# One decode step in full precision: memory values formed by tokens, norm weights on ScalarE, selected value pages loaded by SyncE, and a shorter Newton step in the tail

## The chip, the cores and the metric

The kernel runs on 1 core of one Trainium2 chip. The metric is the device time of one execution in microseconds (us). The time before is the median of three runs.

## What is computed

One layer of a hybrid decoder is applied to 256 prompt tokens (one sequence) and to 32 new tokens (8 sequences of 4), all in float32, with D = 2048. The parts that matter here, cut from the reference:

```python
def rms_norm(x, g):
    y = xf * lax.rsqrt(jnp.mean(xf * xf, axis=-1, keepdims=True) + NORM_EPS)
    return y * g

mkv = (rms_norm(mem_prompt, mem_norm_g[l]) @ w_mem_kv[l]).reshape(1, 256, 2, 4, 128)   # memory keys, values: an output too
h = rms_norm(x, norm_g)
c_h, c_b, c_c, c_g, q, n_g, b_g, kv6, m_q, m_g = split_cols(h @ w_in)
o_cmp, o_sel = nsa_cmp_sel(q, q_rot, pos, k_cmp, v_cmp, k_sel, v_sel)   # v_sel: pages of the cache and new rows
o_m = gqa_attend(m_q, mem_kv[:, :, 0], mem_kv[:, :, 1], None)           # attention over 256 memory tokens
y_m = jax.nn.silu(m_g) * o_m
mixed = jnp.concatenate([y_a, y_b, y_m], axis=-1)
y = rms_norm(x + mixed @ w_out, final_g)
```

The cache of each of the 8 sequences holds 16 pages of 128 tokens, found through a page table.

## The kernel before

**Products.** Every large product is split for precision: a weight "half" (128 x 1024, 512 KB) is copied by ScalarE to a rounded high part (tile `wh`, `w_hi`, L228), VectorE subtracts to get the low part (`wl`, `w_lo`, L233), and TensorE runs 24 matmuls per half: 8 high times high, 8 high times low of the activation, 8 low times high (`product_half`, L250). Two halves make an output tile of 128 columns: weights are the stationary operand and the 256 memory tokens (or 288 tokens of x) stream past them, into a PSUM tile `z`. Raw halves are prefetched five deep (`w_load`, L221): the first 14 on SyncE's queue, all later ones on GpSimd's. All matmuls are recorded as L120, transposes as L125, all VectorE and ScalarE operations as L137, through helpers.

**The order of the work** is written by a Python planner. TensorE's stream is the main program; after every 12 matmuls it calls `chunk()`, which advances the other jobs (generators in `live`): normalization, rotary and softmax steps, and the stream of cache pages (`stage_stream`). A list `stages` gives each page use a due time, and `loading` with the costs in `ISSUE` estimates when a page is there. What comes out is a fixed order on each engine.

**Start.** The memory rows are squared and scaled by `mem_norm_g`, and w_mem's products run first: four tiles of memory keys, then four of memory values (tiles 4 to 7), each tile [128 channels x 256 tokens]. `mem_rstd` (L878) makes the reciprocal root mean square, spread over tokens in `Vc`. Key tiles go from PSUM to `mixed` by ScalarE and are scaled there by VectorE; value tiles are scaled by VectorE straight from PSUM into `mvt` (`mem_tile`, L1016), stored by a DMA (L898) and turned around by two TensorE transposes each (`mvtp`), since the attention needs tokens on partitions; ScalarE copies them to `mixed`.
Meanwhile `prep_x` (L930) makes the high and low parts of the normalized x: one VectorE SCALAR_TENSOR_TENSOR per 128 rows multiplies `rx` by `norm_g` and by the token's factor `rstd_x`, ScalarE writes the high part (`x<-rx`), VectorE subtracts. The first product of x (q, first head) comes right after the last value tile and the small product `bg`.

**The decode caches** pass through six 512 KB page buffers (`st`, and `qk` once the prompt's memory attention is over). SyncE loads compressed-branch pages (`ckc`, 256 KB each), selected keys (`ckk`, 128 KB each), window and memory rows; each page address is read from the page table into a register (`page_ids`, L333). The selected values are different: `selv_load` (L583, recorded as L584) is one GpSimd indirect DMA per 512 KB buffer, that is four pages, with row numbers in `rows_v`; there are 16 such loads for each half of the sequences. Four buffers make one group, used by 16 or more `od` matmuls. A SyncE DMA waits in its order for the one eight before it.

**End.** The first pass of the output projection (`y1`) runs as tiles and as row products `zr`; `split_y1` makes its operands, last the decode columns of the memory heads, and then the second pass. In the tail the last columns are formed by rows: z[0], z[1] for the prompt, and `zd` for the 32 decode tokens (`decode_rows`, L1544). For each of the three, the partial sum is added (`squares`, L1551), squared and summed by ScalarE, and `rsqrt` (L199) turns the sum into the factor r by a square root on ScalarE and a Newton step on VectorE; r is spread by a matmul (`rb`), and the output is scaled and stored (L1571, L1578).

Of the kernel before, what the change touches and what calls it, by code (L numbers as in the profile page):

```python
# [79 lines left out]
def decode_step(ctx, tc, xT, xN, xD, xL, fgl, memT, cst, w_in, w_mem, w_out, w_bg, pt, ptv, ckc, ckk, ckv, wk, wv, mk, mv,  # L80
                o_y, o_kv, o_mem, o_conv, o_wk, o_wv):
# [1680 lines left out]
```

## Time and profile before

| what | value |
|---|---|
| runs | 610.86, 612.21 and 616.13 us (median 612.21) |
| the profiled execution | 616.16 us |
| its span in the profile | 614.4 us |
| granted TensorE clock | 0.996 |
| HBM over the span | 184.74 MB read, 13.60 MB written |
| longest-busy engines after TensorE | VectorE 461.0 us, ScalarE 285.3 us, GpSimd 200.5 us |

In timeline rows the first number is the start in us from the span's start, the second the time up to the end of the row's last instruction, and "x16" counts instructions that the row joins. A bracket at the end gives idle time before the row and what ended it. Matmuls overlap, so their pace is read from start to start. In rows of groups, the numbers behind the bar are total busy us and mean ns of one, then the idle time before them. SPq and POOLq rows are DMA issues on SyncE and GpSimd.

### The profile page before, as it was taken

How to read it: one execution, taken by the hardware profiler on the slowest of the kernel's cores; microseconds unless marked ns; L12 is line 12 of the kernel's file. 1: busy time of each engine (PE TensorE's matmuls, PEld its weight loads, DVE VectorE, ACT ScalarE, POOL GpSimd, SP SyncE). 2: the span in 40 equal slices, each digit the busy share in tenths (PEclk: the TensorE clock that was granted, in tenths of full speed). 3: DMA queues.
4: the chain of work that ended last, by engine and by line, in shares of the span. 5: the costliest groups of instructions: out<-in, count | busy, mean ns of one | idle time of the engine just before them, and what ended most of it. 6: DMA issues, size and time to landing. Idle time of an engine off the chain costs nothing.

```text
span 614.4 us, 13419 instructions
## 1 busy us (share of the span) xinstructions
PE 603.0 (98%) x4919; PEld 554.0 (90%) x4919; DVE 461.0 (75%) x749; ACT 285.3 (46%) x499; POOL 200.5 (33%) x282
## 2 busy tenths in 40 slices
PE   8999999999999999999999999999999999999997
PEld 5999999989799999989889889899889989889995
DVE  4879899988485779989789888897668733357666
ACT  4755445543355444435334434543543544335552
POOL 2012544533124442433453552323111336222200
PEclk8999999999999999999999999999999999999999
DMA  8999798999968999798878898999899998859834
GB/s 285 394 403 404 258 320 300 345 310 337 365 203 280 370 407 375 250 387 298 310 232 313 284 386 273 309 318 311 289 334 332 336 353 291 288 195 411 281 130 155
DMA packets 76226, 190.85 MB, mean 311 GB/s; under 512 B 8896, under 2 KB 26464, under 8 KB 75904
## 3 DMA queue, kind: packets, MB, share of 16 engines
q0 software_dynamic: 26048, 100.48, 46.0%
q1 hardware_dynamic: 49104, 88.25, 40.4%
q10 hardware_dynamic: 1008, 1.25, 0.6%
q8 instruction: 39, 0.64, 0.4%
q14 instruction: 27, 0.22, 0.1%
HBM read 184.74 MB, written 13.60 MB: 323 GB/s over the span
## 4 chain that ended last, share of the span: by engine, by line
PE 78%; DMA 11%; DVE 8%; issue 2%; SPq 1%; ACT 0%; ACTq 0%; DVEq 0%
PE z L120 56%; DMA st<-ckc 5%; PE zr L120 4%; PE od L120 3%; DMA st<-ckk 3%; PE sk L120 3%; PE zf L120 2%; DVE wl L137 2%; DVE pooled L137 2%; PE acc L120 2%; PE s L120 2%; DMA rx<-xT 1%; DVE st L137 1%; PE pt L125 1%; DMA mraw<-memT 1%
## 5 line engine op out<-in xcount | busy, mean ns | idle before, releaser
L120 PE MATMUL z<-x,wh 128*128 128x288 f32 x1664 | 254.4, 302 | 0.0
L137 DVE TENSOR_TENSOR wl<-w,wh 128x1024 fp32r<-128x1024 f32 x147 | 185.7, 1265 | 84.6 <-PE z L120 34.9
L120 PEld LDWEIGHTS z<-x,wh 128*128 128x128 f32 x1664 | 229.7, 188 | 7.8 <-issue 6.1
L137 ACT ACTIVATE wh<-w 128x1024 fp32r<-128x1024 f32 x148 | 154.3, 1052 | 25.1 <-PE z L120 15.4
L120 PE MATMUL z<-x,wl 128*128 128x288 f32 x832 | 127.2, 295 | 0.3 <-DVE wl L137 0.3
L120 PEld LDWEIGHTS z<-x,wl 128*128 128x128 f32 x832 | 115.7, 188 | 0.8 <-DVE wl L137 0.7
L356 POOL TENSOR_TENSOR st<-st,cst 128x512 f32<-128x512 f32 x63 | 69.3, 1102 | 133.8 <-DVE st L137 49.3
L225 POOL DMA_DIRECT2D w<-w_in x104 | 58.2, 560 | 109.1 <-DVE wl L137 82.4
L137 DVE TENSOR_REDUCE pooled<-st 128x16 f32<-128x1024 f32 x63 | 76.2, 1210 | 5.8 <-POOL st L356 5.8
L137 DVE TENSOR_TENSOR st<-st,cst 128x512 f32<-128x512 f32 x63 | 43.3, 688 | 10.9 <-DMA st<-ckc 10.8
L225 POOL DMA_DIRECT2D w<-w_out x32 | 17.5, 550 | 63.0 <-DVE wl L137 43.1
L584 POOL DMA_INDIRECT st<-ckv,rows_v x26 | 27.1, 1042 | 31.9 <-PE od L120 17.4
L137 ACT ACTIVATE P<-P,nm 128x128 f32<-128x128 f32 (+1 forms) x32 | 14.2, 445 | 29.3 <-DVE nm L137 29.3
L120 PE MATMUL z<-m,wh 128*128 128x256 f32 x192 | 27.3, 287 | 0.5 <-DVE mvt L137 0.5
L120 PE MATMUL z<-y,wh 128*128 128x288 f32 x192 | 27.6, 297 | 0.0
L120 PE MATMUL z<-y1a,wh 128*128 128x288 f32 x168 | 26.7, 299 | 0.0
L120 PEld LDWEIGHTS z<-y,wh 128*128 128x128 f32 x192 | 26.3, 188 | 0.1
L120 PEld LDWEIGHTS z<-y1a,wh 128*128 128x128 f32 x168 | 23.6, 188 | 2.1 <-issue 1.2
L120 PEld LDWEIGHTS z<-m,wh 128*128 128x128 f32 x192 | 24.7, 191 | 0.8 <-issue 0.7
L120 PE MATMUL sk<-st,qz 128*32 128x256 f32 x272 | 20.4, 383 | 1.4 <-DMA st<-ckk 1.2
L120 PE MATMUL od<-st,S 128*32 128x256 f32 x256 | 18.7, 382 | 0.0
L120 PE MATMUL zf<-mixed,w 128*128 128x256 f32 x64 | 16.6, 421 | 1.9 <-DVE mixed L137 1.7
(318 smaller groups left out, 716.2 us busy)
## 6 DMA issues: line engine op xcount, KB each, us to landing
w<-w_in POOLq DMA_DIRECT2D x104, 512.0 KB
st<-ckc SPq DMA_DIRECT2D x126, 256.0 KB, 5.8
w<-w_out POOLq DMA_DIRECT2D x32, 512.0 KB
st<-ckk SPq DMA_DIRECT2D x112, 128.0 KB, 5.1
w<-w_mem SPq DMA_DIRECT2D x12, 512.0 KB, 7.1
o_wk<-wk POOLq DMA_DIRECT2D x8, 512.0 KB
o_wv<-wv POOLq DMA_DIRECT2D x8, 512.0 KB
st<-mv SPq DMA_DIRECT2D x7, 512.0 KB, 7.9
```

What stands on the lines that cost most here:

```text
L120: nc.tensor.matmul(out, a, b, **kw)
L125: nc.tensor.transpose(out, a, b)
L137: return getattr(self.engine, name)(*args, **kw)
L225: (nc.gpsimd if s >= ON_SYNC else nc.sync).dma_start(raws[s], wsrc[s])
L356: done.append(eng.tensor_tensor(tm[:, :, kv], tm[:, :, kv], acmp[:, kv].unsqueeze(1).unsqueeze(1).to_broadcast([128, 2, 4, 64]), op=ALU.mu ...
L584: nc.gpsimd.indirect_dma_start(t, None, ckv, bass.IndirectOffsetOnAxis(ap=rows_v[:, j * 4 + b:j * 4 + b + 1], axis=0))
```

## The change

It has six parts.

1. **Memory values by tokens** (`mem_values`). The four value products become one product in two PSUM tiles `zv` [128 tokens x 512 channels]: the memory block is stationary and 512 weight columns stream. A half is 12 matmuls of 128x512 in place of 24 of 128x256. The host lays out w_mem's second half accordingly. ScalarE writes both tiles to `mixed` with the token's factor `mr` as scale; two DMAs store them (`o_memv`, 256 KB each, on GpSimd's queue). The `mvt` multiplications, the eight transposes, their eight copies and four 128 KB stores are gone.
2. **Norm weights of x on ScalarE** (`x_scales`): 16 copies of 128x288 with `norm_g` as a per-partition scale, in place, in six groups, one group per half; VectorE then multiplies a whole group (128x864) by `rstd_x` at once.
3. **Selected values of the first half of the sequences** (`selp_load`): four SyncE DMAs per buffer, each a page's rows to 32 partitions with 4 KB each, in place of one indirect DMA. The second half keeps `selv_load`.
4. **`rsqrt` in the tail**: with constants scaled ahead (`rest` has six columns, one more VectorE operation), the step after the square root takes a reciprocal and two operations in place of a reciprocal and three.
5. **Decode rows**: the partial sum enters `zd` by a matmul with the identity, and ScalarE and VectorE read the PSUM tile; VectorE's addition for g = 2 is gone.
6. **Memory columns of `y1`**: `mem_out` calls the last step of `split_y1` itself, where `split_y1` polled for it before.

```diff
-ISSUE = {"cmp_load": 1.5, "selk_load": 3.75, "selv_load": 0.0}
+ISSUE = {"cmp_load": 1.5, "selk_load": 3.75, "selv_load": 0.0, "selp_load": 3.0}
...
     def rsqrt(r, ssq, rest=None):
 
         v, t = small(3, "yv", 1)[:, :r.shape[1]], small(3, "yt", 1)[:, :r.shape[1]]
-        act.activation(r, ssq, AF.Sqrt, scale=1.0 / D, bias=C("eps") if rest is None else rest)
-        if rest is None:
-            vec.tensor_scalar(v, ssq, 1.0 / D, EPS, op0=ALU.mult, op1=ALU.add)
-        else:
-            vec.scalar_tensor_tensor(v, ssq, 1.0 / D, rest, op0=ALU.mult, op1=ALU.add)
+        if rest is not None:
+            act.activation(r, ssq, AF.Sqrt, scale=1.0 / D, bias=rest[0])
+            vec.scalar_tensor_tensor(v, ssq, -0.5 / D, rest[1], op0=ALU.mult, op1=ALU.add)
+            vec.reciprocal(r, r)
+            vec.scalar_tensor_tensor(t, r, r, v, op0=ALU.mult, op1=ALU.mult)
+            vec.scalar_tensor_tensor(r, t, 1.5, r, op0=ALU.add, op1=ALU.mult)
+            return
+        act.activation(r, ssq, AF.Sqrt, scale=1.0 / D, bias=C("eps"))
+        vec.tensor_scalar(v, ssq, 1.0 / D, EPS, op0=ALU.mult, op1=ALU.add)
         vec.reciprocal(r, r)
         vec.tensor_tensor(t, r, r, op=ALU.mult)
         vec.scalar_tensor_tensor(t, t, -0.5, v, op0=ALU.mult, op1=ALU.mult)
...
         mm.sort(key=lambda x: x[0])
-        for n, (_, a, b) in enumerate(mm):
+        run_half(s, [(out, a, b, first and n == 0, last and n == 23) for n, (_, a, b) in enumerate(mm)], last)
+    def run_half(s, mm, last, between=None):
+        m = len(mm) // 2
+        for n, (out, a, b, start, stop) in enumerate(mm):
             if s == DIRECT and n == 0:
-            if n == LOAD_AT:
+            if n == LOAD_AT * m // 12:
                 w_load(s + WR + 1)
                 next(x_next, None)
-            matmul(out, a, b, start=(first and n == 0), stop=(last and n == 23))
-            if n == 23 and LOW_FIRST <= s < NH - 18:
+                if s > 5:
+                    next(x_scale, None)
+            matmul(out, a, b, start=start, stop=stop)
+            if n == 2 * m - 1 and LOW_FIRST <= s < NH - 18:
                 w_lo(s + 2)
-            if n % 12 == 11 and not (last and n == 23):
+            if n == 7 and between:
+                between()
+            if n == m - 1:
+                chunk()
+            if n == 2 * m - 1 and not last:
                 chunk()
...
+    def mem_values():
+        z = [pz.tile([128, 512], F32, name=f"zv{tt}", tag="z") for tt in range(2)]
+        def out(tt):
+            planes = mixed[:, 12 + 2 * tt:14 + 2 * tt, 0:256]
+            act.activation(planes, z[tt].rearrange("p (a n) -> p a n", a=2), AF.Copy, scale=mr[:, tt:tt + 1])
+            nc.gpsimd.dma_start(o_memv[tt].rearrange("p (a n) -> p a n", a=2), planes)
+
+        for h in range(8):
+            s = nhalf[0]
+            nhalf[0] += 1
+            w_hi(s + 2)
+            w_lo(s + 1)
+            wh, wl = his.pop(s), los.pop(s)
+            mm = []
+            for tt in range(2):
+                for k in range(2):
+                    hi, lo = (m_hl[n][:, 2 * h + k, tt * 128:(tt + 1) * 128] for n in range(2))
+                    w = slice(k * 512, (k + 1) * 512)
+                    early = 2 * tt + (k if h == 7 and tt else 0)
+                    mm += [(early, tt, hi, wh[:, w]), (early, tt, lo, wh[:, w]), (2.5 if h == 7 and not tt else 4, tt, hi, wl[:, w])]
+            mm.sort(key=lambda x: x[0])
+            i = [[n for n, x in enumerate(mm) if x[1] == tt] for tt in range(2)]
+            run_half(s, [(z[tt], a, b, h == 0 and n == i[tt][0], h == 7 and n == i[tt][-1]) for n, (_, tt, a, b) in enumerate(mm)],
+                     h == 7, (lambda: out(0)) if h == 7 else None)
+        assert "rstd_m" in env
+        out(1)
+        chunk()
...
+    def selp_load(j, b, t):
+        src = ckv.rearrange("(a p) c -> a p c", p=32)
+        for i, v in enumerate(page_ids(128 + j * 16 + b * 4, 4)):
+            nc.sync.dma_start(t[32 * i:32 * i + 32, :], src[ds(v, 1)].rearrange("a p c -> (a p) c"))
...
         env["mem_decoded"] = True
+        if "rest" in y1:
+            while env.get("gated", 0) < 4:
+                yield 1
+            y1["rest"]()
...
-    stages += spread(*T_V0, some(winv_load, winv_use, 0, 1) + some(selv_load, selv_use, 0, 4))
+    stages += spread(*T_V0, some(winv_load, winv_use, 0, 1) + some(selp_load, selv_use, 0, 4))
...
+    def x_scales():
+        for i in range(6):
+            yield
+            k, t = xg[i]
+            for j in range(t.shape[1] // NT):
+                act.activation(xr[k + j], xr[k + j], AF.Copy, scale=C("ng")[:, k + j:k + j + 1])
+
+    x_scale = x_scales()
...
+        for i in range(4):
             while i not in mem_raw:
                 yield 1
-            dst = mem_raw[i]
-            if i < 4:
-                vec.tensor_tensor(dst, dst, rstd_m, op=ALU.mult)
-            yield 1
-            if i == 3:
-                nc.gpsimd.dma_start(o_mem[0:4].rearrange("m p n -> p m n"), mkT)
-            if i >= 4:
-                nc.gpsimd.dma_start(o_mem[i], dst)
-                yield 2
-                t = ptr.tile([128, 512], F32, name=f"mvtp{i}", tag="t")
-                for s in range(2):
-                    transpose(t[:, s * 128:(s + 1) * 128], dst[:, s * 128:(s + 1) * 128], ident)
-                for s in range(2):
-                    act.activation(mvn(s, i - 4), t[:, s * 128:(s + 1) * 128], AF.Copy)
+            vec.tensor_tensor(mem_raw[i], mem_raw[i], rstd_m, op=ALU.mult)
+            yield 1
+        nc.gpsimd.dma_start(o_mem.rearrange("m p n -> p m n"), mkT)
...
-        g, r = C("ng"), rstd_x
+        r = rstd_x
         flat = lambda t, k, n: t[:, k:k + n, :].rearrange("p k n -> p (k n)")
         for i in range(len(xg) + 1):
             if i < len(xg):
                 k, x = xg[i]
                 n = x.shape[1] // NT
-                for j in range(k, k + n):
-                    vec.scalar_tensor_tensor(xr[j], xr[j], g[:, j:j + 1], r, op0=ALU.mult, op1=ALU.mult)
+                xv = x.rearrange("p (k n) -> p k n", n=NT)
+                vec.tensor_tensor(xv, xv, r.unsqueeze(1).to_broadcast([128, n, NT]), op=ALU.mult)
                 act.activation(flat(x_hl[0], k, n), x, AF.Copy)
...
     def mem_tile(i, z):
-        dst = mkT[:, i, :] if i < 4 else zt("A", "mvt")[:, :256]
-        if i < 4:
-            act.activation(dst, z, AF.Copy)
-        else:
-            yield 2
-            assert "rstd_m" in env
-            vec.tensor_tensor(dst, z, rstd_m, op=ALU.mult)
-        mem_raw[i] = dst
+        act.activation(mkT[:, i, :], z, AF.Copy)
+        mem_raw[i] = mkT[:, i, :]
+        return
+        yield
...
         then(mem_tile(i, z))
-    for i in range(2, 8):
+    for i in range(2, 4):
         then(mem_tile(i, proj(*m_hl, 256)))
+    mem_values()
...
-        while not env.get("mem_decoded"):
-            yield 1
...
+        def rest():
...
+            y1["done"] = True
+
+        y1["rest"] = rest
+        if env.get("mem_decoded"):
+            rest()
...
                 matmul(zd[32 * q:32 * q + 32, :128], mixed[:, k, 256:NT], wr[k // 2][:, o:o + 128],
-                       start=(k == 0), stop=(k == KT - 1), skip_group_check=True)
-
-    def squares(g, z):
-        vec.tensor_tensor(part[g], z, part[g], op=ALU.add)
-        act.activation(scratch[:, :part[g].shape[1]], part[g], AF.Square, accum_out=sums2[:, g:g + 1])
+                       start=False, stop=(k == KT - 1), skip_group_check=True)
+
+    y_of = [part[0], part[1], zd[:, :128]]
+
+    def squares(g):
+        if g < 2:
+            vec.tensor_tensor(part[g], z[g], part[g], op=ALU.add)
+        act.activation(scratch[:, :part[g].shape[1]], y_of[g], AF.Square, accum_out=sums2[:, g:g + 1])
     def gains(g):
-        vec.tensor_tensor(out[g][:, out[g].shape[1] - part[g].shape[1]:], part[g], fgr[g], op=ALU.mult)
+        vec.tensor_tensor(out[g][:, out[g].shape[1] - part[g].shape[1]:], y_of[g], fgr[g], op=ALU.mult)
         r = small(1, f"yr{g}", 1)
-        rsqrt(r, ssq, rest[:, g:g + 1])
+        rsqrt(r, ssq, (rest[:, g:g + 1], rest[:, 3 + g:4 + g]))
...
+    vec.tensor_scalar(rest[:, 0:3], ssq[:, 0:3], 1.0 / D, EPS, op0=ALU.mult, op1=ALU.add)
+    vec.tensor_scalar(rest[:, 3:6], ssq[:, 0:3], -0.5 / D, -0.5 * EPS, op0=ALU.mult, op1=ALU.add)
+    squares(0)
...
+    matmul(zd[:, :128], ident, part[2], start=True, stop=False, skip_group_check=True)
     decode_rows(0, SPREAD_AT)
...
-    squares(2, zd[:, :128])
```

The planner puts out a new order. The places below are those where it differs most beside the diff.

ScalarE, from the sixth value half on. `wh` is a high weight part, `x` a high part of x, `mixed<-mvtp` a transposed value tile. Before:

```order
L137 ACTIVATE wh_558<-w_411 128x1024
L137 ACTIVATE x_112<-rx 128x864
L137 ACTIVATE wh_603<-w_455 128x1024
L137 ACTIVATE mixed<-mvtp_619 128x128 x2
L137 ACTIVATE x_112<-rx_413 128x864
L137 ACTIVATE wh_651<-w_504 128x1024
L137 ACTIVATE x_112<-rx_457 128x288
L137 ACTIVATE wh_694<-w_552 128x1024
L137 ACTIVATE mixed<-mvtp_710 128x128 x2
L137 ACTIVATE wh_738<-w_595 128x1024
```

After; `rx<-rx,cst` are the copies with `norm_g`, `mixed<-zv` the two value tiles:

```order
L137 ACTIVATE rx_413<-rx_413,cst 128x288 x3
L137 ACTIVATE wh_557<-w_448 128x1024
L137 ACTIVATE x_112<-rx_413 128x864
L137 ACTIVATE rx_450<-rx_450,cst 128x288
L137 ACTIVATE wh_586<-w_484 128x1024
L137 ACTIVATE x_112<-rx_450 128x288
L137 ACTIVATE wh_614<-w_518 128x1024
L137 ACTIVATE wh_640<-w_549 128x1024
L137 ACTIVATE mixed<-zv_427,mr 128x2x256
L137 ACTIVATE mixed<-zv_428,mr 128x2x256
L137 ACTIVATE wh_667<-w_580 128x1024
L137 ACTIVATE bgT<-bg 128x288
```

The weight halves of the first product of x (`wh_614` and `wh_640`) now stand ahead of the two value evictions, and the norm-weight copies between the weight copies.

TensorE, the end of the value products and the first product of x (`z_794`). Before:

```order
L120 MATMUL z_693<-m_111,wh_651 128x256
L120 MATMUL z_693<-m_110,wl_696 128x256 x8
L120 MATMUL bg<-rx_249,qmz 32x288 x3
L120 MATMUL bg<-rx,qmz 32x288 x9
L120 MATMUL bg<-rx_413,qmz 32x288 x3
L120 MATMUL bg<-rx_457,qmz 32x288
L120 MATMUL z_794<-x_112,wh_694 128x288
L120 MATMUL z_794<-x_113,wh_694 128x288
```

After:

```order
L120 MATMUL zv_428<-wh_586,m_110 128x512
L120 MATMUL zv_428<-wh_586,m_111 128x512
L120 MATMUL zv_427<-wl_616,m_110 128x512 x2
L120 MATMUL zv_428<-wh_586,m_110 128x512
L120 MATMUL zv_428<-wh_586,m_111 128x512
L120 MATMUL zv_428<-wl_616,m_110 128x512 x2
L120 MATMUL z_666<-x_112,wh_614 128x288
L120 MATMUL z_666<-x_113,wh_614 128x288
```

The tile `zv_427` ends four matmuls before `zv_428`, and the first product of x (now `z_666`) follows at once; `bg` (16 matmuls) now comes after its first 12 matmuls, where it stood ahead of that product. The four pairs of transposes `mvtp` that stood inside the halves before this place and after it are gone.

The loads of selected values, one buffer group's start. Before, on GpSimd (`w` is a weight load, `st<-st,cst` a multiplication for a compressed page):

```order
L356 TENSOR_TENSOR st_107<-st_107,cst 128x2x256
L225 DMA w_3824<-w_in 128x1024
L584 DMA st_108<-ckv,rows_v 128x1024
L584 DMA st_104<-ckv,rows_v 128x1024
L584 DMA qk_793<-ckv,rows_v 128x1024
L584 DMA st_105<-ckv,rows_v 128x1024
L356 TENSOR_TENSOR st_106<-st_106,cst 128x2x256
L225 DMA w_3900<-w_in 128x1024
L225 DMA w_3965<-w_in 128x1024
```

After, on SyncE, the start of the first of the four buffers (ISA sets up a register):

```order
L387 ISA
L387 DMA st_105<-ckc 128x512
L387 ISA
L387 DMA st_105<-ckc 128x512
L379 TENSOR_LOAD ptt
L631 ISA
L631 DMA st_106<-ckv 32x1024
```

The pair of ISA and DMA comes four times for each buffer, behind one table read. So a group has 16 DMAs in SyncE's order, ahead of the `ckc` pages that follow; GpSimd's order has no `ckv` row until the second half of the sequences.

More of the change, by code (lines that the diff above doesn't have):

```diff
@@ L80, in decode_step @@
 def decode_step(ctx, tc, xT, xN, xD, xL, fgl, memT, cst, w_in, w_mem, w_out, w_bg, pt, ptv, ckc, ckk, ckv, wk, wv, mk, mv,
-                o_y, o_kv, o_mem, o_conv, o_wk, o_wv):
+                o_y, o_kv, o_mem, o_memv, o_conv, o_wk, o_wv):
     nc = tc.nc
@@ L680, in memv_use @@
         yield
+    y1 = {}
     def mem_out():
@@ L771, in decode_step @@
     rstd_m = Vc
+    mr = one.tile([128, 2], F32, name="mr")
     rstd_x = zt("C", "rstd_x")
@@ L917, in token_rstd @@
         yield lag
-        r = small(3, "yr")
         w = len(groups)
@@ L1131, in mem_gate @@
         vec.tensor_scalar(sg_m[:, h, :], sg[:, 256:NT], 0.5, None, op0=ALU.mult)
+        env["gated"] = h + 1
     def nsa_gate(h, z):
@@ L1401, in split_y1 @@
             vec.tensor_tensor(y1["lo"](j)[:, :n], mixed[:, j, :n], y1["hi"](j)[:, :n].bitcast(F32), op=ALU.subtract)
-        while not env.get("mem_decoded"):
-            yield 1
-        m = mixed[:, 4:8, 256:NT]
-        vec.tensor_tensor(m, m, sg_m, op=ALU.mult)
-        act.activation(a[:, 4:8, 256:NT], m, AF.Copy)
-        for lo, j in ((a[:, 12:14, 256:NT], 4), (b[:, :, 256:NT], 6)):
-            vec.tensor_tensor(lo, mixed[:, j:j + 2, 256:NT], a[:, j:j + 2, 256:NT].bitcast(F32), op=ALU.subtract)
-        y1["done"] = True
+        def rest():
+            m = mixed[:, 4:8, 256:NT]
+            vec.tensor_tensor(m, m, sg_m, op=ALU.mult)
+            act.activation(a[:, 4:8, 256:NT], m, AF.Copy)
+            for lo, j in ((a[:, 12:14, 256:NT], 4), (b[:, :, 256:NT], 6)):
+                vec.tensor_tensor(lo, mixed[:, j:j + 2, 256:NT], a[:, j:j + 2, 256:NT].bitcast(F32), op=ALU.subtract)
+            y1["done"] = True
+        y1["rest"] = rest
+        if env.get("mem_decoded"):
+            rest()
     spawn(split_y1(), 2)
@@ L1530, in decode_step @@
     out = (yo[:, 0:2048], yo[:, 2048:4096], yod)
-    rest, sums2 = small(3, "yrest", 1), small(3, "ysums", 1)
+    rest, sums2 = small(6, "yrest", 1), small(3, "ysums", 1)
     quarters = small(32, "imp", 1)
@@ L1600, in decode_step @@
     rows(z[0], ws[2], 6, y, 0, False, True)
-    vec.tensor_scalar(rest, ssq[:, 0:3], 1.0 / D, EPS, op0=ALU.mult, op1=ALU.add)
-    squares(0, z[0])
+    vec.tensor_scalar(rest[:, 0:3], ssq[:, 0:3], 1.0 / D, EPS, op0=ALU.mult, op1=ALU.add)
+    vec.tensor_scalar(rest[:, 3:6], ssq[:, 0:3], -0.5 / D, -0.5 * EPS, op0=ALU.mult, op1=ALU.add)
+    squares(0)
     gains(0)
@@ L1611, in decode_step @@
     scale_tiles(0, 4, 8, nc.sync)
-    squares(1, z[1])
+    squares(1)
     scale_tiles(0, 8, 12, nc.sync)
@@ L1620, in decode_step @@
     scale_tiles(1, 0, 4, nc.sync)
-    squares(2, zd[:, :128])
+    squares(2)
     busy(TAIL_BUSY[0])
@@ L1677, in _ktiles, with _kpairs @@
     return w.reshape(KT, 128, n, 128).transpose(2, 1, 0, 3).reshape(n, 128, KT * 128)
+def _kpairs(w):
+    return w.reshape(4, 4, 128, 512).transpose(0, 2, 1, 3).reshape(4, 128, 2048)
 def _inputs(x_prompt, x_sample, cache_kv, cache_win, state_conv, cache_mem, page_table, mem_prompt,
@@ L1716, in _inputs @@
     pt = np.concatenate([page_table.reshape(2, 4, 8, 2).transpose(0, 2, 1, 3).reshape(1, 128),
-                         page_table.reshape(2, 4, 16).transpose(0, 2, 1).reshape(1, 128)], 1)
+                         page_table.reshape(2, 4, 4, 4).transpose(0, 2, 1, 3).reshape(1, 128)], 1)
     ptv = page_table.reshape(2, 4, 4, 4).transpose(3, 0, 2, 1).reshape(4, 32).repeat(32, 0)
@@ L1720, in _inputs @@
                 memT=A(np.concatenate([vec(mem_norm_g), tr(mem_prompt.reshape(256, D)).reshape(128, KT * 256)], 1)), cst=A(cst), w_in=A(_ktiles(wcat)),
-                w_mem=A(_ktiles(w_mem_kv[0])), w_out=A(np.concatenate([_ktiles(wo[:, :128 * DT]), wl.transpose(0, 2, 1, 3).reshape(4, 128, 2048)], 0)), w_bg=A(wbg), pt=A(pt), ptv=A(ptv), ckc=A(ckc), ckk=A(ckk), ckv=A(ckv),
+                w_mem=A(np.concatenate([_ktiles(w_mem_kv[0][:, :512]), _kpairs(w_mem_kv[0][:, 512:])])), w_out=A(np.concatenate([_ktiles(wo[:, :128 * DT]), wl.transpose(0, 2, 1, 3).reshape(4, 128, 2048)], 0)), w_bg=A(wbg), pt=A(pt), ptv=A(ptv), ckc=A(ckc), ckk=A(ckk), ckv=A(ckv),
                 wk=A(wk), wv=A(wv), mk=A(mk), mv=A(mv))
-_OUTS = dict(o_y=(128, KT * NT), o_kv=(12, 128, NT), o_mem=(8, 128, 256), o_conv=(128, 72), o_wk=(4, 2, 128, 1024),
+_OUTS = dict(o_y=(128, KT * NT), o_kv=(12, 128, NT), o_mem=(4, 128, 256), o_memv=(2, 128, 512), o_conv=(128, 72), o_wk=(4, 2, 128, 1024),
              o_wv=(2, 4, 128, 1024))
@@ L1744, in _outputs @@
             A(kv[:NTP, 4:6])[None, None], A(conv[0:2])[None, None],
-            A(r["o_mem"].reshape(2, 4, 128, 256).transpose(3, 0, 1, 2))[None, None],
+            A(np.stack([r["o_mem"].transpose(2, 0, 1), r["o_memv"].reshape(256, 4, 128)], 1))[None, None],
             A(kv[NTP:, 0:4]).reshape(1, 8, 4, 4, 2, 128), A(win)[None], A(conv[2:18]).reshape(1, 8, 2, 512))
```

6 lines of the change are left out of this document (2 added, 4 removed).

## Prediction

> **What bounds the kernel now.** I read the page's busy table first, then the chain of waits that ended last, then TensorE's waits.
>
> ```profile
> PE 603.0 (98%) x4919; PEld 554.0 (90%) x4919; DVE 461.0 (75%) x749; ACT 285.3 (46%) x499; POOL 200.5 (33%) x282
> PE 78%; DMA 11%; DVE 8%; issue 2%; SPq 1%; ACT 0%; ACTq 0%; DVEq 0%
> ```
>
> ```profile
> PE zf L120 <- DVE mixed L137: 1.7, 2, 1.4
> PE sk L120 <- DMA st<-ckk: 1.2, 1, 1.2
> PE pt L125 <- DVE P L137: 1.2, 1, 1.2
> PE z L120 <- DVE mvt L137: 0.5, 1, 0.5
> ```
>
> TensorE is busy 603.0 of 614.4 us. The rows of its waits show total, count and longest: between the first products and the tail hardly 4 us are waits. So the bound is TensorE's own work, and an edit pays if it takes matmuls out, closes one of these few waits, or shortens the tail behind the last matmul. Work taken from VectorE (75% busy) or GpSimd (33%) pays nothing by itself, and every new wait of TensorE costs its full length.
>
> **Memory values by tokens.** TensorE's timeline over the eight halves of the value products:
>
> ```profile
> 35.87 1.69 PE L120 MATMUL z<-m,wh 128*128 128x256 f32 x12
> 45.03 2.08 PE L120 MATMUL z<-m,wh 128*128 128x256 f32 x16
> 47.91 1.60 PE L120 MATMUL z<-m,wh 128*128 128x256 f32 x12
> 49.35 0.38 PE L125 MATMUL mvtp<-cst,mvt 128*128 128x128 f32 x2
> 51.00 2.08 PE L120 MATMUL z<-m,wh 128*128 128x256 f32 x16
> 52.92 1.18 PE L120 MATMUL z<-m,wl 128*128 128x256 f32 x8
> 54.59 1.66 PE L120 MATMUL z<-m,wh 128*128 128x256 f32 x12 [0.50 <-DVE mvt L137]
> 60.70 2.15 PE L120 MATMUL bg<-rx,qmz 128*32 128x288 f32 x32
> ```
>
> An undisturbed half of 24 matmuls takes 47.91 - 45.03 = 2.88 us, so 0.120 us for each 256-wide matmul. For the 512-wide form the row products near the end give the pace:
>
> ```profile
> 592.62 1.09 PE L120 MATMUL zr<-wh,y 128*128 128x512 f32 x4
> 594.01 1.09 PE L120 MATMUL zr<-wh,y 128*128 128x512 f32 x4
> ```
>
> Six lie between these starts (four of this row and two low ones), so 1.39 / 6 = 0.232 us each. Twelve make 2.78 us: 0.10 less per half, 8 x 0.10 = **0.8 us** in all. Halving the count saves little because the columns streamed stay the same. [...]
>
> The half that starts at 47.91 with a pair of transposes lasts to 51.00, 3.09 us or 0.21 more than one without. Four pairs go: **0.85 us**. The wait before 54.59 goes too: eight matmuls from 52.92 end at 52.92 + 8 x 0.12 = 53.88, so TensorE lost **0.7 us** until VectorE had read a PSUM tile; the new tiles are held through all eight halves and are not read in between. Together 2.35 us off a stretch that now lasts 60.70 - 35.87 = 24.8 us (0.4 of it is transposes that fall after 60.70).
>
> **What stands against it there.** First, the new order on ScalarE: the eviction of `zv_427` stands behind the weight copies for halves 16 and 17, and the first product of x needs that tile's buffer. ScalarE, VectorE and the pace of preparation before:
>
> ```profile
> 44.48 1.22 DVE L137 TENSOR_TENSOR wl<-w,wh 128x1024 fp32r<-128x1024 f32 x1
> 45.62 1.37 DVE L137 SCALAR_TENSOR_TENSOR rx<-rx,cst,rstd_x 128x288 f32<-128x288 f32 x3
> 47.24 1.05 DVE L137 TENSOR_TENSOR x<-rx,x 128x864 fp32r<-128x864 f32 x1
> 58.62 1.06 ACT L137 ACTIVATE wh<-w 128x1024 fp32r<-128x1024 f32 x1
> L137 ACT ACTIVATE ysum<-ysum,cst 128x288 f32<-128x288 f32 x12 | 6.4, 537 | 0.4
> L137 ACT ACTIVATE x<-rx 128x864 fp32r<-128x864 f32 x5 | 4.6, 928 | 7.9 <-DVE rx L137 7.9
> 49.72 0.53 POOL L225 DMA_DIRECT2D w<-w_in  x1 [1.55 <-DVE wl L137]
> ```
>
> The copy at 58.62 is that of half 17; its load was issued at 49.72, so it takes at most 8.9 us to land. With the halves 0.1 to 0.3 us shorter the load goes out near 48.6 and is there by 57.5 at the latest; the copy (1.06) ends by 58.6 and the eviction, 0.63 us for 512 columns like the ScalarE row of 128x512 quoted for the tail, by 59.2. Without a wait the first product of x would start at 60.70 - 0.8 - 0.42 - 0.7 = 58.8 (0.42 for the two transpose pairs before that point). That is a wait of 0 to 0.4 us, more if the load lands later than now; I take **0.3**, bounds 0 and 2.4 (2 us later).
>
> Second, the norm weights. The operation moved is not in the trace of before, but a ScalarE copy of the same shape with a per-partition scale is: 537 ns. Three cost at most 1.6 us, at least 3 x (928 / 864 x 288 = 309 ns) = 0.9. ScalarE then does per half about 1.06 + 0.93 + 1.3 = 3.3 us, and VectorE 1.22 + 1.05 + 1.05 = 3.3 (a 128x864 multiplication taken like the subtraction) where it had 1.22 + 1.37 + 1.05 = 3.6 and in every second half an `mvt`. TensorE needs 2.78 per half. So preparation is quicker than before and still slower than TensorE over the five halves in which it runs, 5 x 0.5 = 2.5 us of drift, against a lead of about two halves (low parts are made one half ahead and weights two). I take **0.2 us** of wait from this, with bounds 0 and 2.
>
> **Selected value pages.** GpSimd loses 16 operations on which TensorE does not wait; no gain. SyncE gets 64 page loads, and the `od` groups are read every 15 to 20 us. These rows show how fast SyncE brings pages now, how long they take to land, and how close the groups stand:
>
> ```profile
> 390.60 7.32 SPq L342 DMA_DIRECT2D st<-ckk  x12
> 425.21 13.73 SPq L342 DMA_DIRECT2D st<-ckk  x16
> 149.82 1.81 SPq L342 DMA_DIRECT2D st<-ckk  x3
> 160.20 1.02 PE L120 MATMUL sk<-st,qz 128*32 128x256 f32 x10 [1.24 <-DMA st<-ckk]
> st<-ckk SPq DMA_DIRECT2D x112, 128.0 KB, 5.1
> 293.48 0.66 PE L125 MATMUL pt<-cst,P 128*128 128x128 f32 x4
> 313.51 0.41 PE L120 MATMUL od<-st,S 128*32 128x256 f32 x2
> 352.30 1.87 PE L120 MATMUL z<-x,wh 128*128 128x288 f32 x12
> 367.55 0.42 PE L120 MATMUL od<-st,S 128*32 128x256 f32 x3
> ```
>
> Twelve key pages went out in 7.32 us (0.61 each), sixteen in 13.73 (0.86), and half of them land within 5.1 us. The first group has from 293.48 to 313.51, 20.0 us, for 16 x 0.61 to 0.86 + 5.1 = 14.9 to 18.9. The last has 367.55 - 352.30 = 15.25 us now; the new order puts 12 fewer 288-wide matmuls there (1.6 us), so 13.65, for 12 pages: 7.3 to 10.3 + 5.1 = 12.4 to 15.4. So the first three groups should be in time and the last is on the edge: I take **0.6 us** of wait, with bounds 0 and the rival below. A value page is 4 KB to each of 32 partitions, which no row shows; by bytes it is one of the key pages.
>
> [...]
>
> **The tail.** Rows from the last matmul to the last store:
>
> ```profile
> 601.72 0.49 PE L120 MATMUL rb<-cst,yr 128*128 128x128 f32 x2
> 599.84 0.63 ACT L137 ACTIVATE st<-ysum 128x512 f32<-128x512 f32 x1 [5.01 <-DVE ysum L137]
> 607.86 0.29 DVE L137 TENSOR_TENSOR ysum<-zd,ysum 128x128 f32<-128x128 f32 x1
> 608.19 0.31 ACT L137 ACTIVATE st<-ysum 128x128 f32<-128x128 f32 x1 [1.18 <-DVE ysum L137]
> 609.91 0.16 DVE L137 SCALAR_TENSOR_TENSOR yt<-yt,yv 128x1 f32<-128x1 f32 x1
> 610.11 0.16 DVE L137 SCALAR_TENSOR_TENSOR yr<-yt,yr 128x1 f32<-128x1 f32 x1
> ```
>
> The addition at 607.86 holds ScalarE's squares until 608.19; without it they start about 0.33 earlier. One Newton operation of the chain goes, 610.11 - 609.91 = 0.20. Against these stands the identity matmul, at most the 0.49 of the two 128x128 `rb` records at 601.72, at least 0.12 by the 256-wide pace; I take 0.2. Sum: 0.33 + 0.20 - 0.2 and about 0.2 from shorter waits of `rb` for the earlier factors: **0.5 us** gained, bounds 0 and 0.8. The last part (memory columns of `y1`) I cost at nothing: TensorE waits there for nothing now, and the row products it still has before those columns cover the chain; without that cover it is four operations of about 0.3 us (rows 607.86 and 608.19 have its size), 1.2 us.
>
> **Sum.** -0.8 - 0.85 - 0.7 + 0.3 + 0.2 + 0.6 - 0.5 = -1.75 us. The profiled 616.16 (span 614.4 and 1.76 around it) becomes 614.4; it ran 3.95 us above the median, so I carry the difference over to the median: 612.21 - 1.75, **610.5 us**.
>
> **Rivals.** (a) *Preparation becomes the bound in the value stretch*: the load of half 17 lands 2 us later than now, or the drift reaches TensorE by as much, so 2.4 in all. For it: this stretch, where VectorE is busy all the time and the DMA engines are full (columns PE, PEld, DVE, ACT, POOL, granted clock, DMA share, GB/s):
>
> ```profile
> 40.00:50.00 10.00, 10.00 (x86) 10.00 (x85) 10.00 (x18) 5.63 (x6) 3.20 (x6) 1.00 1.03 398
> ```
>
> Against it: VectorE's work per half falls. Then -2.35 + 2.4 + 0.6 - 0.5 = +0.15: 612.4.
>
> (b) *Slower: the value pages come late.* The place is `od`; the point is SyncE's pace: above (13.65 - 5.1) / 12 = 0.71 us per page the last group waits, above (20.0 - 5.1) / 16 = 0.93 the first too. The price: the third page row above ended at 151.63 and its user started at 160.20, so a page may need 8.6 us. With that and 0.86, a group of 16 needs 22.4 and one of 12 needs 18.9: late by 2.4 for the first, taken alike for the next two, and by 5.2 for the last, 12.4 us. With the rest (-2.35): 622.3. Against it: 5.1 is the median, and only one key group of the whole run waited, 1.24 us.
>
> (c) *More gain*: the new order also closes the waits of 1.2 and 1.2 for P and for key pages in the list above (GpSimd and VectorE have less ahead of them), and the pages cost nothing: -1.75 - 0.6 - 2.4 = -4.75: 607.5.
>
> (d) *It does not do what it says*: the 512-wide matmuls run no faster per column and the waits stay; only the transposes and the tail are won, -0.85 - 0.5 + 1.1: 612.0.
>
> **Chances.** Forecast 0.48, (a) 0.2, (b) 0.12, (c) 0.12, (d) 0.08. The likeliest case alone spans 609 to 612; 8 in 10 needs (c), (a) and (d), and the near part of (b): **606.3 to 615.5**. A measurement here tells about 1% (6.1 us) from no change, that is below 606.1 or above 618.3. Faster: the lower half of (c), 0.07 with a little from the rest. Slower: three quarters of (b), 0.09. Same: 0.84. [...]
>
> **What would show it.** Right: 12 matmuls `zv<-wh,m` and `zv<-wl,m` per half at 0.23 us from start to start; the first q matmul near 58.5 to 59; no `mvtp`; `od` groups without a wait for DMA, or one short one at the last; ScalarE's last squares directly behind `zd`; TensorE busy near 600.5. Wrong: a wait of `od` for `st<-ckv` over 1 us in each group, a wait of `z` for `wl` or for the eviction over 1 us near 50 to 60 us, or a new wait in the tail at `rb`.

## The result, and the profile after

| | before | changed |
|---|---|---|
| runs | 610.86 to 616.13 us, median 612.23 (10 runs) | 615.68 to 628.4 us, median 620.5 (10 runs) |
| ratio, 95% interval | | 1.0107 (1.0084 to 1.0131) |
| span of the profiled execution | 614.4 us | 620.3 us |

The change made the kernel slower by 1.1% (6.6 us of 612.23), where 1.75 us less was forecast; the measured time lies above the range of 606.3 to 615.5. The ratio leaves out the run of 628.4 us, which counts as slow (granted clock 0.988, the other nine 0.990 to 0.997); the medians of all ten runs differ by 8.3 us. I read the profile after in the same order as the one before: busy times, then TensorE's waits.

```profile
PE 604.1 (97%) x4817; PEld 549.2 (89%) x4817; DVE 454.6 (73%) x732; ACT 292.1 (47%) x509; POOL 185.5 (30%) x264
```

```profile
PE od L120 <- DMA st<-ckv: 8.5, 3, 3.3
PE zf L120 <- DVE mixed L137: 1.2, 2, 1.0
PE zeros L120 <- POOL zeros L885: 1.2, 1, 1.2
PE acc L120 <- DVE pcT L137: 0.7, 1, 0.7
```

The first row of the waits is new and answers most of it: the `od` matmuls, which use the selected values of the first half, waited three times for pages, 8.5 us in all. The old waits for key pages, for P and for `mvt` are not in the list any more.

The value products came out near what the prediction had for them. TensorE's timeline:

```profile
35.08 1.66 PE L120 MATMUL zv<-wh,m 128*128 128x512 f32 x6
41.15 1.98 PE L120 MATMUL zv<-wh,m 128*128 128x512 f32 x8
43.87 1.98 PE L120 MATMUL zv<-wh,m 128*128 128x512 f32 x8
58.03 1.85 PE L120 MATMUL z<-x,wh 128*128 128x288 f32 x12
```

A half takes 43.87 - 41.15 = 2.72 us (0.227 per matmul). From the first value matmul to the first product of x it is 58.03 - 35.08 = 22.95 us, where it was 24.83 up to `bg`: 1.9 us less, and 0.4 us of transposes less behind it.

The loss lies in the page stretch. Rows of TensorE at the first, third and fifth `od` groups, and what comes behind the last:

```profile
286.48 1.93 PE L120 MATMUL od<-st,S 128*32 128x256 f32 x32
329.55 1.89 PE L120 MATMUL od<-st,S 128*32 128x256 f32 x26 [3.10 <-DMA st<-ckv]
368.21 0.76 PE L120 MATMUL od<-st,S 128*32 128x256 f32 x2 [2.12 <-DMA st<-ckv]
372.26 0.61 PE L120 MATMUL od<-st,S 128*32 128x256 f32 x1 [3.29 <-DMA st<-ckv]
375.59 0.80 PE L120 MATMUL z<-x,wh 128*128 128x288 f32 x4
```

and the same two ends in the profile before:

```profile
291.61 1.07 PE L120 MATMUL od<-st,S 128*32 128x256 f32 x16
369.42 0.80 PE L120 MATMUL z<-x,wh 128*128 128x288 f32 x4
```

From the first `od` group (window values) to the product behind the fifth it is 375.59 - 286.48 = 89.1 us, and was 369.42 - 291.61 = 77.8: **11.3 us more**. Before that stretch the changed trace was 5.1 us ahead, behind it 6.2 us late. So the whole loss and more is there. (Of the lead, 0.8 us was there at the first value matmul already, 35.08 against 35.87; the traces of the experiments start it anywhere between 34.71 and 36.64, so that part belongs to the single execution.)

The granted clock shows a second part of it. Columns of these stretches: PE, PEld, DVE, ACT, POOL busy, granted TensorE clock, DMA share, GB/s.

```profile
322.00:331.00 9.00, 5.90 (x61) 4.88 (x60) 4.79 (x12) 3.37 (x7) 0.53 (x1) 1.00 1.03 296
368.00:372.00 4.00, 0.76 (x2) 0.14 (x2) 0.00 (x0) 0.00 (x0) 0.00 (x0) 0.56 1.02 288
372.00:374.00 2.00, 1.74 (x20) 0.96 (x24) 0.71 (x2) 0.00 (x0) 0.00 (x0) 0.50 1.02 365
374.00:376.00 2.00, 2.00 (x17) 0.93 (x10) 1.20 (x2) 0.73 (x4) 1.63 (x2) 0.67 0.53 170
```

The clock fell to half behind the wait of 2.12 us and stayed there through the next one: a mean of 0.56 over 368 to 372 is 0.50 with some 0.5 us of full clock ahead of it, so it fell near 368.5, and by the 0.67 of the last row it came back near 375.3. So the rest of the last group ran at half pace: from 372.26 to 375.59, 3.3 us for 26 matmuls that take about 1.5 at full clock (at the fourth group 32 take 350.92 - 349.05 = 1.87). The length of a wait alone does not tell when this comes: the clock fell after 2.12 us without a matmul, and stayed at 1.00 around the wait of 3.10 us at the third group (first row).

How the pages came, in rows of SyncE:

```profile
287.18 11.21 SPq L631 DMA_DIRECT2D st<-ckv  x16
304.57 17.36 SPq L631 DMA_DIRECT2D st<-ckv  x16
331.07 11.01 SPq L631 DMA_DIRECT2D st<-ckv  x16
347.61 1.85 SPq L631 DMA_DIRECT2D qk<-ckv  x4
351.00 13.52 SPq L631 DMA_DIRECT2D st<-ckv  x12
```

The last twelve went out in 13.52 us, 1.13 us each, and the last of them was used at 372.26, 7.7 us after the issues ended at 364.52. Sixteen went out at the forecast pace twice (0.70 and 0.69 each), and the groups that use them did not wait; the second sixteen (1.08 each) and the last twelve belong to the two groups that did. The DMA engines were not idle: in a window of 13 us over the first group (packets, MB and share of 16 engines for each queue; q1 is SyncE's, q0 GpSimd's; the last number of a load's row is the median time from issue to landing),

```profile
q1 hardware_dynamic: 914, 2.27, 69.3%
q0 software_dynamic: 294, 1.06, 28.9%
st<-ckv SPq DMA_DIRECT2D x16, 128.0 KB, 6.4
```

they were taken to 98% and moved 258 GB/s. SyncE's queue (the pages and a few `ckc` loads) got 2.27 MB for 0.693 x 16 x 13 = 144 us of engine time: 15.7 GB/s for each busy engine. In the profile before, a window of 13 us over sixteen key pages has this:

```profile
q1 hardware_dynamic: 2318, 2.37, 57.5%
```

2.37 MB for 120 us: 19.8 GB/s. So a byte in pages of the new shape took a quarter more engine time. Why is the question of the experiments.

### The profile page after: what moved, and what is told of

Read it like the earlier page. It is cut to its first block, busy times and chain, and to the rows that moved or that the text cites. A ratio compares the mean times of both kernels' runs of the same rounds, so it can differ in the third digit from the quotient of the medians.

```text
span 620.3 us, 13428 instructions
## 1 busy us (share of the span) xinstructions
PE 604.1 (97%) x4817; PEld 549.2 (89%) x4817; DVE 454.6 (73%) x732; ACT 292.1 (47%) x509; POOL 185.5 (30%) x264
## 4 chain that ended last, share of the span: by engine, by line
PE 82%; DMA 11%; DVE 3%; SPq 1%; issue 1%; ACT 0%; ACTq 0%; DVEq 0%
PE z L120 58%; DMA st<-ckv 6%; PE zr L120 4%; PE zv L120 4%; PE sk L120 3%; PE od L120 3%; DMA qk<-ckc 3%; PE zf L120 2%; DMA st<-ckc 2%; PE acc L120 1%; PE s L120 1%; DVE pooled L137 1%; DMA mraw<-memT 1%; SPq L631 1%; PE om L120 1%
## 5 line engine op out<-in xcount | busy, mean ns | idle before, releaser
L137 DVE TENSOR_TENSOR wl<-w,wh 128x1024 fp32r<-128x1024 f32 x147 | 183.2, 1249 | 72.3 <-PE z L120 42.9
L401 POOL TENSOR_TENSOR st<-st,cst 128x512 f32<-128x512 f32 x56 | 63.1, 1127 | 137.7 <-DVE st L137 88.1
L137 DVE TENSOR_REDUCE pooled<-st 128x16 f32<-128x1024 f32 x56 | 67.8, 1211 | 3.1 <-POOL st L401 3.1
L137 DVE TENSOR_TENSOR st<-st,cst 128x512 f32<-128x512 f32 x56 | 38.3, 685 | 26.3 <-DMA st<-ckc 26.3
L120 PE MATMUL od<-st,S 128*32 128x256 f32 x288 | 22.3, 399 | 8.5 <-DMA st<-ckv 8.5
L120 PEld LDWEIGHTS od<-st,S 128*32 128x32 f32 x288 | 10.2, 113 | 16.8 <-issue 7.9
L137 ACT ACTIVATE se<-z 128x288 f32<-128x288 f32 x16 | 6.5, 408 | 30.6 <-PE z L120 30.6
L634 POOL DMA_INDIRECT st<-ckv,rows_v x14 | 14.1, 1007 | 17.3 <-PE od L120 11.6
L401 POOL TENSOR_TENSOR qk<-qk,cst 128x512 f32<-128x512 f32 x8 | 9.1, 1137 | 31.5 <-issue 17.0
```

The source lines that it names most:

```text
L120: nc.tensor.matmul(out, a, b, **kw)
L137: return getattr(self.engine, name)(*args, **kw)
L401: done.append(eng.tensor_tensor(tm[:, :, kv], tm[:, :, kv], acmp[:, kv].unsqueeze(1).unsqueeze(1).to_broadcast([128, 2, 4, 64]), op=ALU.mu ...
L634: nc.gpsimd.indirect_dma_start(t, None, ckv, bass.IndirectOffsetOnAxis(ap=rows_v[:, j * 4 + b:j * 4 + b + 1], axis=0))
```

## The experiments

**Theory P**: a load to 32 adjacent partitions is slow on the DMA engines because of where it lands. **Rival Q**: SyncE's queue takes one load after the other with few under way, whatever the place. **Rival D**: it is the size or the number of the rows in a load. Ratios are against the kernel before in the same job, where its median was 615.2 (the first four), 615.0 (the next four) and 613.7 us (the last three).

**1. Indirect loads back.** Only part 3 is undone:

```diff
-    ... some(selp_load, selv_use, 0, 4))
+    ... some(selv_load, selv_use, 0, 4))
```

> The changed kernel with only the selected value pages of the first half put back on GpSimd's indirect loads; the other five parts stay. Both theories on why the pages come late (P: 32 adjacent partitions take only part of the DMA engines' rate; Q: SyncE's queue takes one load after the other, whatever the place) expect the od matmuls to wait for no DMA again. The changed trace was 5.2 us ahead of the trace of before when the first od group started (286.48 against 291.68) and won 0.44 us in the tail, so: 612.2 - 5.6 = 606.6 us, between 605 and 609. A third reading, that the other parts cost time too, expects 611 or more.

Measured: 612.0 us, ratio 0.994 (0.9909 to 0.9971), no wait of `od` for a page. The other five parts together are a gain of 0.6%, 3.7 us at the ratio (1.8 to 5.6); the 5.6 us that I expected rested on one trace's lead and is the far end of that. The time itself lies where the third reading had it (611 or more), but that bound was worked out from 612.2 us for the kernel before, which took 615.2 in this job; the ratio speaks against that reading. Part 3 is what made the kernel slower.

**2. Every fourth partition.** Same order on all engines, same loads, another place:

```diff
-            nc.sync.dma_start(t[32 * i:32 * i + 32, :], src[ds(v, 1)]...)
+            nc.sync.dma_start(t[i:128:4, :], src[ds(v, 1)]...)
```

> The changed kernel, every instruction in the same place, but a value page goes to every fourth partition (32 rows of 4 KB to partitions i, i+4, ..., i+124) in place of 32 adjacent ones. The rows land in other places than the weights expect, so the decode attention over selected values of the first half is another sum; the work is the same. P expects the waits of od for st<-ckv (8.5 us) and the slow od matmuls behind them (about 2 us) to go: 609 to 612 us, and DMA rate in the page stretches back from about 255 to over 300 GB/s. Q expects no change: 619 to 622 us.

Measured: 612.94 us, ratio 0.9963 (0.9937 to 0.999). One wait of `od` is left, 2.7 us at the last group. The window of 13 us over the first group:

```profile
q1 hardware_dynamic: 928, 2.30, 51.9%
st<-ckv SPq DMA_DIRECT2D x16, 128.0 KB, 3.2
```

2.30 MB for 108 us, 21.3 GB/s per busy engine, and half of the loads landed within 3.2 us where it was 6.4. Q is refuted: queue, number, order and row size (4 KB) are the same, and only the place differs. The rate over all queues did not rise above 300 GB/s, as P had it, but in one of the four page stretches (263, 313, 265 and 285). What fell is the time that the engines needed: the two queues took 77% of the window where it was 98%. The weight loads on GpSimd's queue ran faster too in this one window (1.11 MB at 25.5%, 20.9 GB/s, where the changed kernel has 17.6).

**3. Pages as 128 rows of 1 KB.** A page goes to all partitions, into a quarter of the buffer's columns; the weights' transposes take contiguous columns:

```diff
-            nc.sync.dma_start(t[32 * i:32 * i + 32, :], src[ds(v, 1)]...)
+            nc.sync.dma_start(t[:, i * 256:(i + 1) * 256], src[ds(v, 1)]...)
...
-        parts = w.rearrange("p (r c) -> p c r", c=4)
+        parts = w.rearrange("p (c r) -> p c r" if q and hf == 0 else "p (r c) -> p c r", c=4)
```

> The changed kernel with a value page as 128 rows of 1 KB to all 128 partitions, a quarter of the buffer's columns each; the transposes of the weights take contiguous columns for it, and the result is the same. Loads, queue and order are the same, rows per load are four times as many. P expects 607 to 612 us and od without waits over 1 us. Q expects 619 to 622 us. A third theory, D (the loads are slow by the size or number of their rows), expects it to be slower than the changed kernel, 622 or more, since rows are shorter.

Measured: 610.14 us, ratio 0.9919 (0.9886 to 0.9952). No `od` waits. Its window and its last group:

```profile
q1 hardware_dynamic: 2375, 2.42, 59.5%
st<-ckv SPq DMA_DIRECT2D x16, 128.0 KB, 4.0
```

```profile
346.44 8.91 SPq L631 DMA_DIRECT2D st<-ckv  x12
360.76 0.42 PE L120 MATMUL od<-st,S 128*32 128x256 f32 x3
```

2.42 MB for 124 us, 19.6 GB/s per engine, and the last twelve went out in 8.91 us. D is refuted in the form that shorter rows make it slower. Against the changed kernel this is 1.9% faster (0.9919 against 1.0107, from two jobs), with one load's shape changed.

**4. Pages as 64 rows of 2 KB** on 64 adjacent partitions:

```diff
-            nc.sync.dma_start(t[32 * i:32 * i + 32, :], ...)
+            h, g = divmod(i, 2)
+            nc.sync.dma_start(t[64 * g:64 * g + 64, h * 512:(h + 1) * 512], ...)
```

> The changed kernel with a value page as 64 rows of 2 KB to 64 adjacent partitions (0 to 63 or 64 to 127); same loads, same queue, same result. [...] P in a plain form, in which the rate grows with the number of partitions, expects about halfway, 613 to 616. Q expects 619 to 622 us.

Measured: 618.68 us, ratio 1.005 (1.0024 to 1.0076); `od` waited three times, 5.4 us in all. The window of the first group:

```profile
q1 hardware_dynamic: 1326, 2.23, 61.0%
```

2.23 MB for 127 us: 17.6 GB/s. The time lies above the 613 to 616 of P in the plain form, but the ratio, taken of the 612.2 us that the bounds were worked out from, is 615.3 and lies inside; so this run does not decide whether the rate grows with the number of partitions. It is slow, a little less so than 32 partitions (1.0107, and 1.0088 in run 5, whose interval overlaps). Its loads alternate between the two halves of the partitions, those of the changed kernel come in pairs; run 6 tries the order by itself.

**5. The changed kernel again**, for the same job as the next three.

> The changed kernel as it is, for comparison on the same chip as the next three. All theories expect about 1.01 of the time before again, with 8 to 10 us lost between the third and the fifth od group.

Measured: 620.91 us, ratio 1.0088 (1.0046 to 1.013); this profiled execution waited once, 4.2 us, at the fourth group, and its `od` matmuls behind that took 3.50 us where 26 take about 1.5. From the first group to the product behind the fifth it is 371.74 - 288.65 = 83.1 us, 5.3 more than before the change, where I expected 8 to 10. So in two executions of one kernel different groups were late, and the loss in that stretch was 11.3 and 5.3 us.

**6. Alternating halves.** The four loads of a buffer go to partitions 0-31, 64-95, 32-63, 96-127, in this order:

```diff
-        for i, v in enumerate(page_ids(128 + j * 16 + b * 4, 4)):
+        vs = page_ids(128 + j * 16 + b * 4, 4)
+        for i in (0, 2, 1, 3):
```

> The changed kernel with the four loads of a buffer issued in the order of partitions 0-31, 64-95, 32-63, 96-127, so that neighbours in the queue go to different halves of the partitions; sizes and number are the same, same result. P in the form that several loads are under way and share their halves expects an improvement: waits of od for st<-ckv halved, 613 to 617 us. P in the form that every load by itself runs at a reduced rate, whatever its neighbour does, expects no change against the changed kernel: within 2 us of it, and 15 to 16 GB/s per busy DMA engine on SyncE's queue as there.

Measured: 618.76 us, ratio 1.0053 (1.0024 to 1.0081); `od` waited 3.6 us in two pieces. The window:

```profile
q1 hardware_dynamic: 902, 2.28, 60.9%
```

2.28 MB for 127 us: 18.0 GB/s. In this window it is the rate of the 64 partitions above, and the time is the same too, so the order can account for their small advantage as well as the number. But the rate does not hold: over the four value groups of this trace it is 18.0, 15.0, 17.6 and 15.6 GB/s, and 15.8 to 16.6 in the changed kernel (table at the end). A gain in rate by alternating is not shown, nor one in time, since the interval overlaps that of run 5. Most of the slowness stays when neighbours in the queue go to different halves; that fits the second of my two forms better.

**7. Both halves of the sequences** with 128 rows of 1 KB:

```diff
-    ... some(selv_load, selv_use, 1, 4))
+    ... some(selp_load, selv_use, 1, 4))
```

> Value pages as 128 rows of 1 KB (the form that came out fastest) for the second half of the sequences too, no indirect load left. If GpSimd's indirect loads cost TensorE nothing in the second half, the time stays within 1 us of the form with the first half alone, about 0.992 of the time before. If page loads on SyncE come late there too (its od groups stand 7 to 10 us apart, and 16 loads need about 10.7 us), od waits by 2 to 4 us a group: 8 to 12 us slower than that, about 1.005 to 1.01.

Measured: 609.98 us, ratio 0.9932 (0.9901 to 0.9962). No page is late, and it is the same as run 3 within the intervals (some 0.3% each way): a cost of the indirect loads of the second half is not seen.

**8. Part 3 alone** on the kernel before.

> The kernel before with part 3 alone (first half's value pages by four SyncE loads each to 32 adjacent partitions). P expects the whole loss here: 1.015 to 1.02 of the time before, od waiting 6 to 12 us for st<-ckv. A rival, that the loss arises only because the other parts bring the od groups closer or fill the queues, expects under 1.005.

Measured: 629.06 us in four runs, ratio 1.0214 (1.0152 to 1.0277). Here `od` waited 7.5 us for value pages, and a key page came 3.0 us late too. The loss needs none of the other parts. With them it is 1.1% smaller, where run 1 gave them a gain of 0.6%; the intervals allow both to be one number.

**9. Run 3 again**, as the base of the last two.

> The changed kernel with value pages as 128 rows of 1 KB again, as the base for the next two on the same chip: 0.990 to 0.995 of the time before, no wait of od for a page.

Measured: 610.47 us, ratio 0.9928 (0.9902 to 0.9954), as expected.

**10. Norm weights back on VectorE** (part 2 undone in that base): the loop of SCALAR_TENSOR_TENSOR in `prep_x` is back and `x_scales` is not called.

> The base with part 2 taken back: the norm weights of x are multiplied by VectorE again, three operations per group. In the changed trace VectorE ended the low parts for the last two value halves only 0.15 us before TensorE read them (53.91 against 54.05, 56.38 against 56.52), and the old form costs it 1.37 - 1.06 = 0.3 us more per half, five times. So TensorE should wait for wl near 50 to 60 us, 1.0 to 1.6 us in all, and the time be 1 to 2 us above the base. If the lead is larger than it looks there is no wait, and the time is the same.

Measured: 611.52 us, ratio 0.9967 (0.9947 to 0.9988); at the ratios 2.4 us above the base, with intervals that just touch, and 1.05 at the medians. The trace shows the expected waits:

```profile
51.52 1.21 PE L120 MATMUL zv<-wl,m 128*128 128x512 f32 x4 [0.38 <-DVE wl L137]
54.91 1.20 PE L120 MATMUL zv<-wl,m 128*128 128x512 f32 x4 [0.34 <-DVE wl L137]
58.96 1.86 PE L120 MATMUL z<-x,wh 128*128 128x288 f32 x12
```

Its value products began at 34.87, so they took 24.09 us against 22.95: 1.1 us. So part 2 is what lets part 1 keep its gain; part 2 without part 1 was not run.

**11. Values by channels again** (part 1 undone in that base): `proj` for tiles 4 to 7, `mvt`, transposes and copies are back.

> The base with part 1 taken back: four value tiles by 24 matmuls of 256 columns per half, with VectorE's multiplications, the eight transposes and their copies. By the prediction's terms it loses 0.8 (shorter matmuls) + 0.85 (transposes) + up to 0.7 (the wait for the PSUM tile): 1.6 to 2.4 us above the base, first product of x near 60 us in the trace. If the part is worth nothing, within 0.5 us.

Measured: 613.2 us, ratio 1.0007 (0.9973 to 1.004): 4.8 us above the base at the ratios, more than the 1.6 to 2.4 expected, with intervals of some 2 us either way, and 2.7 at the medians: four of the twelve runs took 617.9 to 619.3 us, the others 610.8 to 614.8, and what sets the four apart is open. In the trace the value products took from 35.81 to 59.88, 24.07 us: 1.1 more than 22.95, with 0.4 for the later transposes, and without the wait for `mvt` that the kernel before had (probably because VectorE has less to do beside it). The rest is elsewhere: this execution waited 2.0 us once for VectorE's `pc`, which the base did not. Whether that belongs to the order that the planner then makes, or to the single execution, was not tried.

## Why the prediction was wrong

**The step that failed** is the cost of the value pages. I wrote that a value page is "by bytes ... one of the key pages" and took 0.6 us of wait. The loads measured 15.7 GB/s per busy engine where key pages have 19.8 and the same 4 KB rows on spread partitions 21.3. With that two of the four value groups were not in time: 8.5 us of waits where the sum had 0.6, and about 1.8 us of half clock where it had nothing. That is 10.3 of the 11.3 us on the stretch; the last 1 us was not broken down. Runs 1, 3 and 8 show that part 3 carries the loss, and run 2 that the place of the rows does.

What let it pass is that the load was priced by its 128 KB alone, with no row of its shape behind it. Runs 4 and 6 (16.3 to 17.8 and 15.0 to 18.0 GB/s, far from 21.3) show that neither 64 adjacent partitions nor neighbours in the queue on different halves bring the rate back. What in the hardware makes the place matter was not shown; the runs show the effect of the place.

**The rival (b)** named this place and price: 622.3 us, with late groups. I gave it 0.12, because only one key group of the old trace had waited. Its mechanism was right in the landing times (7.7 us after the last issue, 8.6 in the rival) and in the issue pace falling behind 0.71 us (1.08 and 1.13 at the groups that waited). What it did not have is the reason: the place of the rows, on 32 adjacent partitions, was in no row of that trace. The clock falling after a wait was in no rival. That 622.3 lies near the measured time is in part luck: the rival had four late groups and 12.4 us of waits, the trace two and 8.5, and the slow matmuls made up some of the difference.

**Right terms.** The shorter matmuls: 0.227 us each, a half 0.16 us shorter where 0.10 was forecast. Transposes and the wait for `mvt` are gone; 1.9 us up to the first product of x and 0.4 behind it are 2.3 together, where the terms less those two waits gave 1.85. The forecast wait at the first product of x (0.3) did not come: half 17's copy was done before the value tile.

```profile
54.75 1.99 ACT L137 ACTIVATE wh<-w 128x1024 fp32r<-128x1024 f32 x2
57.29 0.69 ACT L137 ACTIVATE mixed<-zv,mr 128x512 f32<-128x512 f32 x1 [0.55 <-PE zv L120]
```

The eviction at 57.29 waited for TensorE, not for the weights. The drift did come, in the last two value halves:

```profile
52.03 1.97 PE L120 MATMUL zv<-wh,m 128*128 128x512 f32 x8
55.09 1.55 PE L120 MATMUL zv<-wh,m 128*128 128x512 f32 x6
52.77 1.22 DVE L137 TENSOR_TENSOR wl<-w,wh 128x1024 fp32r<-128x1024 f32 x1
```

They took 3.06 and 2.94 us (to 58.03) where the others take 2.72, 0.56 in all, since the low parts were ready just then (52.77 + 1.22 = 53.99, used at 54.05). The sum had 0.3 for the first product's wait and 0.2 for the drift: 0.5 together, right only as a total, by luck. Run 10 shows 1.1 us more of it with 0.3 us more per half on VectorE.

**The tail** went as the sum had it. Rows before, then after:

```profile
591.22 1.09 PE L120 MATMUL zr<-wh,y 128*128 128x512 f32 x4
607.73 0.80 PE L120 MATMUL idl<-y 128*128 128x288 f32 x4
611.34 0.33 SPq L1578 DMA_DIRECT2D o_y<-yod  x1
```

```profile
597.57 1.09 PE L120 MATMUL zr<-wh,y 128*128 128x512 f32 x4
609.67 0.38 PE L120 MATMUL zd<-ysum,cst 128*128 128x128 f32 x2
614.17 0.79 PE L120 MATMUL idl<-y 128*128 128x288 f32 x4
614.30 0.28 ACT L137 ACTIVATE st<-zd 128x128 f32<-128x128 f32 x1 [1.20 <-PE zd L120]
617.25 0.33 SPq L1635 DMA_DIRECT2D o_y<-yod  x1
```

From the end of `zd` (614.17) to the last store it is 3.08 us, and was 611.34 - 607.73 = 3.61: 0.53 less. The identity matmul takes 0.31 (609.67 to 609.98, where the next matmul starts), and 0.2 was forecast. From the first `zr` of the tail to the last store the trace has 617.25 - 597.57 = 19.68 us against 611.34 - 591.22 = 20.12: 0.44 won, 0.5 forecast. That it is these parts was read from the trace; they were not undone one by one. The memory columns of `y1` cost nothing, as forecast: the list of waits after has no entry for them.

**Rival (c)** was half right: the old waits for key pages and P are gone in the changed trace. But run 1 has a wait of 1.5 us for P again, so such waits come and go with the execution and are no gain to count on.

A version that beats both kernels is run 3 (and run 7): the change with pages as 128 rows, 0.9919 of the time before.

## What to carry to other kernels

A load's cost on the DMA engines depended here on which partitions it fills (15.7 GB/s per busy engine on 32 adjacent ones, 21.3 on every fourth), so bytes and number of loads do not price it: when a change moves a load to another shape, look for a row of that shape, and where none exists treat its pace as unknown. Before taking loads off one queue, work out the pace that the tightest gap allows (here 0.71 us per page) and ask what happens at half that rate. And where TensorE is the bound, price a wait of a few us with the slow matmuls that can follow it (here 3.3 us for 26 that take about 1.5 at full clock).

## What the runs showed of the hardware that was not expected

With the same bytes on the same queue, SyncE's loads ran at these rates per busy engine, over windows of 13 us from the first issue of a value group (10 us for the last group):

| where a page's rows go | four groups, GB/s |
|---|---|
| 32 adjacent partitions (changed kernel) | 15.8, 16.0, 16.1, 16.6 |
| the same, run 5 | 16.5, 16.1, 15.6, 15.4 |
| the same, halves alternating (run 6) | 18.0, 15.0, 17.6, 15.6 |
| 64 adjacent partitions (run 4) | 17.8, 16.8, 16.8, 16.3 |
| 128 partitions, rows of 1 KB (run 3) | 19.8, 20.4, 19.8, 19.9 |
| every fourth partition (run 2) | 21.1, 22.6, 21.2, 21.7 |

Even so the last was not the fastest kernel: in run 2 SyncE sent the sixteens of pages out at 0.77 to 0.86 us each (12.3 to 13.7 us) where in run 3 it sent them at 0.67 to 0.69 (10.7 to 11.1); why the loads with fewer rows went out slower there stays open.
